# Two transformer blocks on one core: weights with adjacent column blocks, a later way back of the expert pairs, and row parts made without a copy

## The chip, the cores and the metric

The kernel runs on one core of a Trainium2 chip. The metric is the time of one execution in microseconds of device time; the runs shown are three, and their median is used. A core has TensorE (PE, with PEld for its weight loads), VectorE (DVE), ScalarE (ACT), GpSimd (POOL) and SyncE (SP), which here issues nearly all DMA transfers.

## The reference, cut to what matters

A first block (stick-breaking attention and a spatial gating unit, then a mixture of 32 experts) is followed by a second block (differential attention, sparse attention, a cross attention over a memory, and a table of 16384 small experts). There are 256 tokens of width 1024, all in 32-bit floats. What the change touches most is the mixture:

```python
def hierarchical_moe(x, ...):                      # x: 256 rows, normed
    ...                                            # top-1 group of 4, then top-2 of its 8 experts, for each token
    for g in range(N_GROUPS):                      # 4
        h = jax.nn.silu(jnp.einsum('nd,edf->nef', xt, w_gate[g])) * jnp.einsum('nd,edf->nef', xt, w_up[g])
        out = out + jnp.einsum('nef,efd->nd', h * combine[:, g, :, None], w_down[g])
```

An expert has `w_gate` and `w_up` of 1024 x 512 and `w_down` of 512 x 1024, 2 MiB each.

## The kernel before, in words

The program is written in program order against tiles with a fixed number of buffers; a planner orders the instructions of each engine by its own estimates and gives out the buffers, and `after(a, b)` makes it keep `a` behind `b` on an engine.

Weights come by SyncE in tiles of 128 x 2048 floats (1 MiB): `queue` lists them, `fill` (L86) issues a load whenever there is room, `next_w` (L128) takes the next one. In the expert stage 11 such tiles are in rotation (pools of 7, 3 and 1). The first pair has three of its tiles in `act` buffers and two in the `hi` and `lo` buffers besides.

Routing (L521 to L613): the rows `X` are scaled by `rs` into `xs` (ACT, L536), copied to the rounded upper part `xsh` (ACT, L537), and the rest `xsl` is taken by POOL (L538). In `route`, DVE makes the masks, PE counts slots (L585, L586), and `slots` (L615) builds `P`, a 0/1 matrix that says which token sits in which of an expert's 64 places. `slots` builds it in two halves of four experts.

Experts (`moe`, L688): four groups g of eight experts, each as four pairs. For each group `gather` (L706) multiplies `xsh` and `xsl` by `P`, which gives the experts' inputs `xe` transposed, in eight blocks of 128 columns of the model width; `gather(0)` serves the first two pairs and stands ahead of the group, `gather(1)` stands in the second pair. Each pair then has: gate and up, 64 matmuls of 512 columns into the `acc` banks (L757; two experts side by side, 64 columns of the array each); `mo_s` from both (ACT L760, DVE L761); four transposes (L765) and the copy `mo_h` (ACT L767); 32 down matmuls into the `oacc` banks (L779); the parts `yh` (ACT L787) and `yl` (DVE L788); and the way back (L789 to L796), eight matmuls with `PT`, the transposed `P`, and four additions to `X` on DVE. `yh`, `yl`, `P` and the parts of other weights share the `hi` and `lo` buffers, three each. PSUM scratch is `wk`, four banks. `memory` (L801) is worked off in pieces behind the pairs 2 to 6 and brings four weight tiles of its own.

The contraction index is laid out so that partition q holds the rows 8q to 8q+7 of a weight (`_cols`, L1686). So the matching block k of the activations has the columns k, 8+k, 16+k and so on, and is read with a step of 8 elements ("(q k) -> k q"): L206 (`xpair`), L644, L703 and L704 (`vh`, `vl`, the stationary operand of the gather) and L1362 (`peer`). For `w_down`, with four blocks, `sv` (L764) is read with a step of 4. Other weights (`_rows`, L1692) already have adjacent blocks.

Of the kernel before, what the change touches and what calls it, by code (L numbers as in the profile page):

```python
# [17 lines left out]
ALU = mybir.AluOpType  # L18
# [24 lines left out]
class _Kernel:  # L43
# [180 lines left out]
    def norm_rows(self, rows, rs, dst):  # L224
        for j in range(2):
            self.nc.vector.tensor_scalar(dst[:, j, :], rows[:, j, :], rs[:, j:j + 1], None, op0=ALU.mult)
# [89 lines left out]
    def phase_a(self):  # L316
# [231 lines left out]
    def route(self, lg):  # L548
# [39 lines left out]
        self.P = {0: self.slots(0)}  # L588
# [26 lines left out]
    def slots(self, g):  # L615
# [3 lines left out]
        for e in range(0, 8, 4):  # L619
            for j in range(2):  # L620
# [6 lines left out]
    def overflow(self):  # L627
# [9 lines left out]
        with tc.If(n > CAP):  # L637
# [6 lines left out]
            xr = xs.rearrange("p j (q k) -> p j k q", k=8)  # L644
# [5 lines left out]
            with tc.For_i(0, 32, 1) as e:  # L650
# [13 lines left out]
                for j in range(2):  # L664
# [4 lines left out]
                    sv = s.rearrange("p (f k) -> p k f", k=4)  # L669
# [18 lines left out]
    def moe(self):  # L688
# [9 lines left out]

        for g in range(4):
# [3 lines left out]
            vh = self.xsh.rearrange("p j (q k) -> p j k q", k=8)  # L703
            vl = self.xsl.rearrange("p j (q k) -> p j k q", k=8)  # L704
# [40 lines left out]
            for pr in range(4):  # L745
                p = g * 4 + pr
                ps = {}
                for nm in ("w_gate", "w_up"):
                    ps[nm] = self.acc()
                    for kh in range(2):  # L750
# [3 lines left out]
                        for k in range(4):  # L754
                            for e in range(2):
                                s0 = (pr * 2 + e) * CAP
                                nc.tensor.matmul(ps[nm][e * 64:(e + 1) * 64, :], lhsT=xe[kh][:, k, s0:s0 + CAP],  # L757
                                                 rhs=w[e][:, k, :], start=(kh + k == 0), stop=(kh * 4 + k == 7))
# [4 lines left out]
                sv = s.rearrange("p (f k) -> p k f", k=4)  # L763
# [25 lines left out]
                for hf in range(2):  # L789
                    sl = slice(hf * 512, (hf + 1) * 512)  # L790
# [962 lines left out]
```

## Time and profile before

| what | before |
|---|---|
| three runs, us | 1798.29, 1800.45, 1802.6; median 1800.45 |
| the profiled execution, us | 1797.24 |
| its span, us | 1795.5 |
| mean granted TensorE clock | 0.988 |
| PE / DVE / ACT / POOL busy | 96% / 55% / 38% / 17% |
| moved by DMA | 410 MB, mean 228 GB/s |
| expert stage | 141.2 to 674.1 us of the span |

How to read it: times are counted from the span's start. A busy share says how long an engine had at least one instruction under way, not that it ran at its peak; matmuls overlap, so that the distance between two starts tells more than the duration of one. A wait names the instruction that waited and the one that released it; "issue" is time without a wait that the trace shows. PEld loads a stationary operand while PE works on the one before. `out<-in` gives the tiles by the program's names, for a matmul the moving operand first, then the stationary one. In tables by stretch the columns are: the stretch, its length, then busy time with the number of instructions in brackets for PE, PEld, DVE, ACT and POOL, then the granted clock of TensorE as a share of 2.4 GHz, the mean busy share of the 16 DMA engines, and what they moved.

### The profile page before, as it was taken

Reading aid. Unit: us, or ns where it says so; the run is one execution under the profiler, and the core shown is the slowest. Engines: PE = TensorE matmul, PEld = TensorE weight load, DVE = VectorE, ACT = ScalarE, POOL = GpSimd, SP = SyncE. Lnnn points to the kernel's source line nnn. Section 1 sums busy time; section 2 is a strip of 40 time slices with the busy share of each in tenths; the row PEclk is TensorE's granted clock in tenths of the full one; section 3 lists DMA queues with packets and bytes.
Section 4 is the critical chain, followed back from the end, with each engine's and each line's share of the span. In section 5 each row is a group of like instructions: output and inputs, shape, how many; then the busy total and the mean of one; then the engine's idle time right before and its main releaser. Section 6 shows DMA issues by size and latency. Waiting matters only on the chain. (4 is left out here: it accounts for less than half of the span.)

```text
span 1795.5 us, 27447 instructions
## 1 busy us (share of the span) xinstructions
PE 1718.2 (96%) x11096; PEld 1354.5 (75%) x11096; DVE 982.3 (55%) x2008; ACT 683.0 (38%) x1150; POOL 309.9 (17%) x178
## 2 busy tenths in 40 slices
PE   8999999999999998999999889999999999999998
PEld 7984445544434438888989889999999978888886
DVE  5462232212212116667566999999999944444444
ACT  6551121111101115546455444544444444444443
POOL 4321000000000005321537620000000022222221
PEclk9998999999999999999999989999999999999999
DMA  9527898898999978352215444444444455565553
GB/s 371 216 110 287 322 415 338 351 382 359 381 416 382 388 325 328 127 212 91 99 38 176 141 144 156 150 157 147 160 165 146 165 175 200 190 232 200 188 188 117
DMA packets 69250, 410.02 MB, mean 228 GB/s; under 512 B 9216, under 2 KB 9856, under 8 KB 28544
## 3 DMA queue, kind: packets, MB, share of 16 engines
q1 hardware_dynamic: 67840, 406.64, 60.4%
q8 instruction: 88, 1.44, 0.3%
q10 hardware_dynamic: 1280, 1.59, 0.2%
q14 instruction: 42, 0.34, 0.1%
HBM read 406.11 MB, written 2.10 MB: 227 GB/s over the span
## 5 line engine op out<-in xcount | busy, mean ns | idle before, releaser
L145 ACT ACTIVATE hi<-w 128x1024 fp32r<-128x1024 f32 x368 | 388.9, 1060 | 504.5 <-PE oa L155 176.9
L146 DVE TENSOR_TENSOR lo<-w,hi 128x1024 fp32r<-128x1024 f32 x260 | 327.2, 1260 | 222.0 <-ACT hi L145 221.7
L146 POOL TENSOR_TENSOR lo<-w,hi 128x1024 fp32r<-128x1024 f32 x108 | 267.2, 2476 | 1018.4 <-ACT hi L145 928.0
L155 PE MATMUL acc<-act,lo 128*128 128x256 f32 x928 | 267.0, 288 | 5.8 <-DVE lo L146 5.8
L153 PE MATMUL acc<-act,hi 128*128 128x256 f32 x928 | 266.3, 287 | 2.4 <-ACT hi L145 1.3
L154 PE MATMUL acc<-act,hi 128*128 128x256 f32 x928 | 264.0, 285 | 0.0
L757 PE MATMUL acc<-w,act 128*64 128x512 f32 x1016 | 246.6, 597 | 0.0
L154 PE MATMUL acc<-lo,act 128*128 128x256 f32 (+1 forms) x592 | 197.1, 333 | 3.0 <-POOL lo L146 1.6
L155 PE MATMUL acc<-hi,act 128*128 128x256 f32 (+1 forms) x592 | 195.8, 333 | 0.2 <-DVE act L1265 0.2
L155 PEld LDWEIGHTS acc<-act,lo 128*128 128x128 f32 x928 | 178.1, 192 | 9.3 <-DVE lo L146 6.6
L153 PEld LDWEIGHTS acc<-act,hi 128*128 128x128 f32 x928 | 178.3, 192 | 6.3 <-ACT hi L145 2.2
L153 PE MATMUL acc<-hi,act 128*128 128x256 f32 (+1 forms) x592 | 177.7, 335 | 1.8 <-ACT act L1608 1.0
L154 PEld LDWEIGHTS acc<-act,hi 128*128 128x128 f32 x928 | 178.3, 192 | 1.4 <-issue 1.2
L757 PEld LDWEIGHTS acc<-w,act 128*64 128x64 f32 x1016 | 73.3, 137 | 135.2 <-issue 131.3
L153 PE MATMUL oa<-act,hi 128*128 128x256 f32 x528 | 151.8, 288 | 4.0 <-ACT hi L145 3.9
L155 PE MATMUL oa<-act,lo 128*128 128x256 f32 x528 | 152.7, 289 | 0.0
L154 PE MATMUL oa<-act,hi 128*128 128x256 f32 x528 | 150.8, 286 | 0.0
L1498 DVE SCALAR_TENSOR_TENSOR oha<-cols,iT,g 128x384 bf16<-128x384 bf16 x256 | 142.3, 612 | 0.0
L154 PEld LDWEIGHTS acc<-lo,act 128*128 128x128 f32 x592 | 114.1, 193 | 16.5 <-DVE lo L146 3.5
L153 PEld LDWEIGHTS acc<-hi,act 128*128 128x128 f32 x592 | 114.1, 193 | 13.3 <-ACT act L1608 1.2
L155 PEld LDWEIGHTS acc<-hi,act 128*128 128x128 f32 x592 | 113.8, 193 | 10.6 <-DVE act L1265 0.4
L779 PE MATMUL oa<-w,mo_h 128*64 128x512 f32 x480 | 113.1, 599 | 5.0 <-ACT mo_h L767 5.0
(424 smaller groups left out, 2587.6 us busy)
## 6 DMA issues: line engine op xcount, KB each, us to landing
w<-w_gate SPq DMA_DIRECT2D x64, 1024.0 KB, 8.5
w<-peer_u SPq DMA_DIRECT2D x64, 1024.0 KB, 4.9
w<-peer_v SPq DMA_DIRECT2D x64, 1024.0 KB, 4.9
w<-w_up SPq DMA_DIRECT2D x63, 1024.0 KB, 9.5
w<-w_down SPq DMA_DIRECT2D x60, 1024.0 KB, 8.7
w<-w_in SPq DMA_DIRECT2D x28, 1024.0 KB, 9.2
w<-w_out SPq DMA_DIRECT2D x8, 1024.0 KB, 16.1
w<-peer_wq SPq DMA_DIRECT2D x8, 1024.0 KB, 4.8
```

Source lines behind the costliest of these rows:

```text
L145: self.last_hi = nc.scalar.activation(hi, src, AF.Copy)
L146: r = (nc.gpsimd if gp else nc.vector).tensor_tensor(lo, src, _f(hi), op=ALU.subtract)
L153: first = mm(ps, lhsT=a[0], rhs=b[0], start=start, stop=False)
L154: mm(ps, lhsT=a[0], rhs=b[1], start=False, stop=False)
L155: return first, mm(ps, lhsT=a[1], rhs=b[0], start=False, stop=stop)
L757: nc.tensor.matmul(ps[nm][e * 64:(e + 1) * 64, :], lhsT=xe[kh][:, k, s0:s0 + CAP], rhs=w[e][:, k, :], start=(kh + k == 0), stop=(kh * 4 + ...
L779: nc.tensor.matmul(y[hf][e * 64:(e + 1) * 64, :], lhsT=hT[:, kh * 2 + k, e * 64:(e + 1) * 64], rhs=w[e][k][:, hf * 512:(hf + 1) * 512], st ...
L1498: V.scalar_tensor_tensor(ab[:, t], cols[:, None, :].to_broadcast([128, 3, 128]), iT[:, t0 + t:t0 + t + 1], g3[:, :, t0 + t:t0 + t + 1].to_ ...
```

## The change

Three edits. First, the host lays every weight out by `_cols`, now with partition q of block k holding row 128k + q; `_rows` is gone, `w_gate`, `w_up`, `w_down`, `w_gb_2` and `peer_u_2` are permuted to match, and the gains are turned (`turned`; `final_norm_g` has a second copy, `final_norm_gk`). On the chip each "(q k)" becomes "(k q)" and each "(f k)" becomes "(k f)": blocks of 128 adjacent columns. Shapes and numbers of the transfers stay. (`norm_rows` and `softmax_rows` are renamed.) Second, the way back of a pair is kept in `late` and issued in the next pair: its first half (columns 0 to 511) behind the last up matmul and ahead of the transposes of `mo_s`, its second half behind the transposes, both pinned there with `after`; the last pair's stands behind the loop. Third, `xs` is gone: `xsh` is made by one scaled ACT copy of `X`, and `xsl` by DVE from `X`, `rs` and `xsh`, pinned between the two halves of the first `P`.

```diff
@@ xpair; the same edit in overflow, moe (vh, vl) and peer
-        r = rows.rearrange("p j (q k) -> p j k q", k=8)
+        r = rows.rearrange("p j (k q) -> p j k q", k=8)
@@ phase_a
-        xs = self.act().rearrange("p (j d) -> p j d", j=2)
...
         for j in range(2):
-            nc.scalar.activation(xs[:, j], X[:, j], AF.Copy, scale=rs[:, j:j + 1])
-            nc.scalar.activation(self.xsh[:, j], xs[:, j], AF.Copy)
-            nc.gpsimd.tensor_tensor(self.xsl[:, j], xs[:, j], _f(self.xsh[:, j]), op=ALU.subtract)
-        self.route(lg)
+            nc.scalar.activation(self.xsh[:, j], X[:, j], AF.Copy, scale=rs[:, j:j + 1])
+        self.route(lg, rs)
@@ route
-        self.P = {0: self.slots(0)}
+        def low():
+            for j in range(2):
+                z = V.scalar_tensor_tensor(self.xsl[:, j], self.X[:, j], rs[:, j:j + 1], _f(self.xsh[:, j]),
+                                           op0=ALU.mult, op1=ALU.subtract)
+                self.after(z, self.last_P)
+
+        self.P = {0: self.slots(0, low)}
@@ slots
         for e in range(0, 8, 4):
+            if e and between:
+                between()
@@ moe
+        late = []
+
+        def back_to(yh, yl, PT, pr, hf, after=None):
+            sl = slice(hf * 512, (hf + 1) * 512)
+            for j in range(2):
+                bk = self.wk()
+                lt = PT[:, pr, j * 128:(j + 1) * 128]
+                mm = nc.tensor.matmul(bk, lhsT=lt, rhs=yh[:, sl], start=True, stop=False)
+                if after:
+                    self.after(mm, after)
+                after = nc.tensor.matmul(bk, lhsT=lt, rhs=yl[:, sl], start=False, stop=True)
+                nc.vector.tensor_tensor(X[:, j, sl], X[:, j, sl], bk, op=ALU.add)
+            return after
...
+                if late:
+                    mm = back_to(*late, 0, mm)
                 pt = self.wk()
-                sv = s.rearrange("p (f k) -> p k f", k=4)
+                sv = s.rearrange("p (k f) -> p k f", k=4)
                 for k in range(4):
-                    nc.tensor.transpose(pt[:, k * 128:(k + 1) * 128], sv[:, k, :], self.ident)
+                    tr = nc.tensor.transpose(pt[:, k * 128:(k + 1) * 128], sv[:, k, :], self.ident)
+                    if late and not k:
+                        self.after(tr, mm)
                 ht = self.tmp([128, 512], "mo_h")
                 nc.scalar.activation(ht, pt, AF.Copy)
+                if late:
+                    back_to(*late, 1, tr)
...
-                for hf in range(2):
-                    sl = slice(hf * 512, (hf + 1) * 512)
-                    for j in range(2):
-                        bk = self.wk()
-                        lt = PT[:, pr, j * 128:(j + 1) * 128]
-                        nc.tensor.matmul(bk, lhsT=lt, rhs=yh[:, sl], start=True, stop=False)
-                        nc.tensor.matmul(bk, lhsT=lt, rhs=yl[:, sl], start=False, stop=True)
-                        nc.vector.tensor_tensor(X[:, j, sl], X[:, j, sl], bk, op=ALU.add)
+                late = yh, yl, PT, pr
                 if 0 <= p - M0 < 5:
                     next(memory)
+        for hf in range(2):
+            back_to(*late, hf)
@@ _cols (the old body of _rows; _rows goes)
-    return np.ascontiguousarray(w.reshape(128, k // 128, m // n, n).transpose(2, 0, 1, 3)).reshape(m // n, 128, -1)
+    return np.ascontiguousarray(w.reshape(k // 128, 128, m // n, n).transpose(2, 1, 0, 3)).reshape(m // n, 128, -1)
@@ layout
+    turned = lambda g: c(g.reshape(8, 128).T).reshape(-1)
...
-        r[n] = a[n].reshape(32, 128, -1)
+        r[n] = c(a[n].reshape(32, -1, 128, a[n].shape[-1]).transpose(0, 2, 1, 3)).reshape(32, 128, -1)
```

## Rows read from the trace of the kernel before

**Rows 1.** Busy us by group of pairs; last columns granted clock, DMA share, GB/s

```profile
141.20:271.90 130.70, 128.17 (x586) 61.95 (x587) 33.48 (x73) 21.94 (x40) 3.15 (x2) 0.98 0.85 339
271.90:417.30 145.40, 139.78 (x667) 72.08 (x665) 28.26 (x47) 20.59 (x34) 8.17 (x3) 1.00 0.91 362
417.30:545.30 128.00, 122.73 (x520) 55.90 (x520) 25.22 (x45) 13.34 (x24) 0.00 (x0) 0.99 0.94 383
545.30:674.10 128.80, 121.86 (x520) 55.68 (x521) 25.59 (x43) 16.38 (x28) 2.28 (x1) 1.00 0.89 360
```

**Rows 2.** Waits of PE and PEld, 140 to 675 (us in total, times, longest)

```profile
PE wk L765 <- DVE mo_s L761: 12.0, 13, 0.9
PE oa L779 <- ACT mo_h L767: 5.0, 7, 0.7
...
PEld wk L794 <- ACT yh L787: 11.5, 15, 0.8
...
PEld acc L757 <- DMA w<-w_down: 0.8, 3, 0.3
```

**Rows 3.** Timeline of one plain pair (start us, duration us, engine, line)

```profile
492.57 13.95 PE L757 MATMUL acc<-w,act 128*64 128x512 f32 x62
...
506.63 0.75 DVE L761 SCALAR_TENSOR_TENSOR mo_s<-acc,mo_c,mo_s 128x512 f32<-128x512 f32 x1 [12.63 <-PE acc L757]
...
507.43 0.75 PE L765 MATMUL wk<-ident,mo_s 128*128 128x128 f32 x4 [0.92 <-DVE mo_s L761]
...
508.93 7.14 PE L779 MATMUL oa<-w,mo_h 128*64 128x512 f32 x32 [0.75 <-ACT mo_h L767]
...
519.38 13.95 PE L757 MATMUL acc<-w,act 128*64 128x512 f32 x62
```

**Rows 4.** Ten us of that pair, columns as in Rows 1

```profile
510.00:520.00 10.00, 10.00 (x44) 4.05 (x41) 3.32 (x6) 1.19 (x2) 0.00 (x0) 1.00 1.02 424
```

**Rows 5.** Weight loads by shape, 140 to 675 (busy us, mean ns, idle before)

```profile
L713 PEld LDWEIGHTS wk<-P,act 128*128 128x128 f32 x128 | 37.1, 338 | 0.0
...
L795 PEld LDWEIGHTS wk<-yl,mo_PT 128*128 128x128 f32 x64 | 10.6, 188 | 8.9 <-DVE X L796 3.2 <-DVE yl L788 2.7 <-issue 1.6
...
L765 PEld LDWEIGHTS wk<-ident,mo_s 128*128 128x128 f32 x64 | 9.0, 209 | 24.4 <-DVE mo_s L761 23.4 <-issue 0.8
...
L730 PEld LDWEIGHTS wk<-ident,P 128*128 128x128 f32 x32 | 3.7, 143 | 0.0
```

**Rows 6.** Timeline of a gather's loads and of contiguous matmuls

```profile
473.56 0.58 PEld L711 LDWEIGHTS wk<-P,act 128*128 128x128 f32 x2
474.04 0.58 PEld L713 LDWEIGHTS wk<-P,act 128*128 128x128 f32 x2
...
386.04 0.28 PE L154 MATMUL acc<-lo,act 128*128 128x256 f32 x1
386.15 0.28 PE L155 MATMUL acc<-hi,act 128*128 128x256 f32 x1
```

**Rows 7.** A wait of ACT in 240 to 430

```profile
ACT hi L145 <- PE wk L794: 2.1, 1, 2.1
```

**Rows 8.** Timeline of POOL and DVE ahead of the first gather

```profile
136.12 4.65 POOL L538 TENSOR_TENSOR act<-act,act 128x1024 fp32r<-128x1024 f32 x2 [4.59 <-ACT act L537]
...
136.26 2.29 DVE L579 TENSOR_TENSOR msk<-oh,oh 128x64 f32<-128x64 f32 x1
...
139.56 1.82 DVE L621 TENSOR_TENSOR P<-iota,slot 128x256 fp32r<-128x256 f32 x2
...
141.52 0.76 DVE L621 TENSOR_TENSOR P<-iota,slot 128x256 fp32r<-128x256 f32 x2
```

**Rows 9.** Timeline of SyncE's weight loads near the stage's start

```profile
125.84 2.03 SPq L122 DMA_DIRECT2D w<-w_gate  x4
155.55 4.24 SPq L122 DMA_DIRECT2D w<-w_up  x4
```

**Rows 10.** Ten us around that gather, columns as in Rows 1

```profile
470.00:480.00 10.00, 9.09 (x33) 6.38 (x33) 1.72 (x3) 2.01 (x4) 0.00 (x0) 0.83 1.01 422
```

More of the change, by code (lines that the diff above doesn't have):

```diff
@@ L222, in flip, with norm_cols @@
         return r
-    def norm_rows(self, rows, rs, dst):
+    def norm_cols(self, rows, rs, dst):
         for j in range(2):
@@ L546, in queue_pair, with route @@
             self.queue(w[a], pool=at.get(a))
-    def route(self, lg):
+    def route(self, lg, rs):
         nc, V = self.nc, self.nc.vector
@@ L613, in route, with slots @@
         V.tensor_copy(self.most, most[:1])
-    def slots(self, g):
+    def slots(self, g, between=None):
         P = self.hl.tile([128, 1024], F32R, tag="hi", name=self.nm("P"), bufs=self.n_hi)
@@ L643, in overflow @@
             nc.vector.tensor_tensor(xs, _f(self.xsh), _f(self.xsl), op=ALU.add)
-            xr = xs.rearrange("p j (q k) -> p j k q", k=8)
+            xr = xs.rearrange("p j (k q) -> p j k q", k=8)
             for k in range(8):
@@ L702, in moe @@
             xe = [self.act().rearrange("p (k s) -> p k s", k=4) for _ in range(2)]
-            vh = self.xsh.rearrange("p j (q k) -> p j k q", k=8)
-            vl = self.xsl.rearrange("p j (q k) -> p j k q", k=8)
+            vh = self.xsh.rearrange("p j (k q) -> p j k q", k=8)
+            vl = self.xsl.rearrange("p j (k q) -> p j k q", k=8)
             def gather(hf):
@@ L756, in moe @@
                                 s0 = (pr * 2 + e) * CAP
-                                nc.tensor.matmul(ps[nm][e * 64:(e + 1) * 64, :], lhsT=xe[kh][:, k, s0:s0 + CAP],
-                                                 rhs=w[e][:, k, :], start=(kh + k == 0), stop=(kh * 4 + k == 7))
+                                mm = nc.tensor.matmul(ps[nm][e * 64:(e + 1) * 64, :], lhsT=xe[kh][:, k, s0:s0 + CAP],
+                                                      rhs=w[e][:, k, :], start=(kh + k == 0), stop=(kh * 4 + k == 7))
                 s = self.tmp([128, 512], "mo_s")
@@ L838, in gains_c @@
         a, self.g2 = [self.cst.tile([128, 8], F32, tag="g_" + nm, name="g_" + nm) for nm in ("mix", "2")]
-        for g, nm in ((a, "norm_mix_2"), (self.g2, "final_norm_g")):
+        for g, nm in ((a, "norm_mix_2"), (self.g2, "final_norm_gk")):
             self.nc.scalar.dma_start(g, self.I[nm].rearrange("(p k) -> p k", k=8))
@@ L902, in phase_c @@
         rsb2 = rsb[:, None, :].to_broadcast([128, 2, 256])
-        self.norm_rows(xs, r1, X)
+        self.norm_cols(xs, r1, X)
         self.save("X", lambda o: nc.sync.dma_start(o.rearrange("(j p) d -> p j d", p=128), X))
@@ L1688, in _cols @@
     k, m = w.shape
-    return np.ascontiguousarray(w.reshape(128, k // 128, m // n, n).transpose(2, 0, 1, 3)).reshape(m // n, 128, -1)
-def _rows(w, n):
-    k, m = w.shape
     return np.ascontiguousarray(w.reshape(k // 128, 128, m // n, n).transpose(2, 1, 0, 3)).reshape(m // n, 128, -1)
@@ L1704, in layout @@
         r[n] = a[n].reshape(-1)
+    turned = lambda g: c(g.reshape(8, 128).T).reshape(-1)
+    r["final_norm_gk"] = turned(r["final_norm_g"])
+    for n in ("attn_norm_g", "ffn_norm_g", "norm_mix_2", "norm_mem_2", "norm_ffn_2"):
+        r[n] = turned(r[n])
     r["mix_norm_g"] = c(np.concatenate([a["sb_out_norm_g"].reshape(-1), a["sg_out_norm_g"].reshape(-1)])
@@ L1722, in layout @@
     r["w_in_2"] = _cols(np.concatenate([w[:, :o[3]], qb, kv, w[:, o[6]:]], axis=1))
-    r["w_gb_2"] = c(w[:, o[5]:o[6]]).reshape(128, -1)
+    r["w_gb_2"] = _cols(w[:, o[5]:o[6]], 24)[0]
     for n in ("nsa_ck_w1_2", "nsa_cv_w1_2"):
@@ L1729, in layout @@
     for n in ("w_branch_a_2", "w_cross_o_2"):
-        r[n] = _rows(a[n][0], 512)
-    r["w_branch_b_2"] = _rows(a["w_branch_b_2"][0].reshape(2, 4, 64, D).transpose(1, 0, 2, 3).reshape(512, D), 512)
-    r["w_out_2"] = _rows(a["w_out_2"][0], 256)
-    r["w_cross_q_2"] = _rows(a["w_cross_q_2"][0], 256)
+        r[n] = _cols(a[n][0], 512)
+    r["w_branch_b_2"] = _cols(a["w_branch_b_2"][0].reshape(2, 4, 64, D).transpose(1, 0, 2, 3).reshape(512, D), 512)
+    r["w_out_2"] = _cols(a["w_out_2"][0], 256)
+    r["w_cross_q_2"] = _cols(a["w_cross_q_2"][0], 256)
     r["w_cross_kv_2"] = _cols(a["w_cross_kv_2"][0])
```

16 lines of the change are left out of this document (8 added, 8 removed).

## The prediction

> **What bounds the kernel now.** I read the table by stage first [rows 1]. The expert stage (141.2 to 674.1 us: four expert groups of four pairs, 532.9 us) is where two of the three edits lie; the stages before and behind it keep their work. PE is busy over 94% of it, and the DMA engines 85 to 94%: two limits close together, and the forecast turns on both. Which one rules now is in the waits [rows 2]: PE's weight loader waited 0.8 us for weights from memory in all, but the transposes waited 12.0 us for `mo_s`, the down matmuls 5.0 us for `mo_h`, the way back's weight loads 11.5 us for `yh`. So PE sets the pace, and the transfers follow it. Then one plain pair, with neither gather nor memory work in it [rows 3]: 62 gate and up matmuls from 492.57, transposes at 507.43, down at 508.93, the way back behind its end at 516.07, next pair at 519.38. The pair takes 26.81 us; 12 weight tiles of 1 MiB at the full rate (424 GB/s at a share of 1.02, [rows 4]) take 12 x 2.473 = 29.7 us. Plain pairs already outrun the transfers and live on the 11 tiles of buffer; the pairs with gathers and memory work let the transfers catch up.
>
> **Column blocks adjacent.** On the chip this changes no size, no count and no DMA: the host permutes rows of the weights, and blocks that were read with a step of 8 floats (`vh`, `vl`, rows in `xpair`, `peer`) or 4 floats (`sv`) become runs of 128. What gets cheaper is the weight load of TensorE where such a block is stationary. The gather is the large one: 128 + 128 matmuls of 256 columns, with a weight load of 338 ns; the way back's loads, same type and size but contiguous, take 188 ns [rows 5]. In sequence, a gather's loads go in pairs 0.48 us apart (473.56, 474.04), so 0.24 us for one matmul; contiguous matmuls of the same 256 columns start 0.11 to 0.12 us apart (386.04, 386.15) [rows 6]. 256 x (0.24 - 0.115) = 32 us of PE. The eviction (0.47 us for each four matmuls, two engines in turns) doesn't limit: four matmuls will take 0.46. Bounds: 0, if the step is not why the loads are long, to 256 x 0.135 = 35. I take 32, since the type and the tile are equal in both rows and only the step differs. The 64 transposes of `mo_s` have loads of 209 ns against 143 for those of `P` [rows 5]; in sequence 0.14 against about 0.115, so 64 x 0.025 = 1.6 us (0 to 4). The Trainium skill (SBUF — State Buffer, the note on cachelines under Door 1: The DMA port swizzle) says that reads are at full speed while two hits fall on one 16-byte line, so that a step of 4 floats is free and one of 8 is not. For the gather that is what the row shows; for `mo_s` the row (209 against 143) speaks against it, and by the page these 1.6 us would be 0. The other transposes, 16 each in four places outside the stage, lie beside evictions of 0.47 us a block; I count them at nothing, 2 us at most if the evictions weren't there.
>
> **Way back pinned into the next pair.** The same 128 matmuls, 64 adds on DVE and no DMA; they only move, in the queues of PE and DVE alone (SyncE's and POOL's are not passed). Removed: down ends at 516.07, the next pair's long run starts at 519.38, and of that 0.43 is two early gate matmuls. With the block gone, gate matmuls follow down at once (the two `acc` banks were read long before). So 3.1 us less. Put back: four matmuls (about 0.23 each, twice 256 columns) between the last up matmul and the transposes, four behind these. Now the gap from the end of up (492.57 + 13.95 = 506.52) to down (508.93) is 2.41 us, with 0.5 of transposes in it [rows 3]. The first four take 0.92 while DVE makes `mo_s` (it lasts 0.75), the last four 0.92 while ACT copies `mo_h`: 1.84 of work into 1.9 us of waiting. Down starts as before; the pair gains the 3.1. What this needs: the four `wk` banks, of which the fifth user waits for the first add of DVE (0.64 us each); DVE's queue has `mo_s` first, then four adds, and nobody waits for the last ones. Not every pair has the whole gap: in about seven, gathers or the memory's matmuls fill part of it already (13 of 16 transposes waited for `mo_s`, only 7 for `mo_h`, [rows 2]). 9 x 3.1 + 7 x 0.5 = 31, less a price: `yh` and `yl` now hold a slot of three for most of a pair more, and the splits of the memory's weights and the next `P` need the same slots. One split already waited 2.1 us for a way back [rows 7]; four such blocks come, so 1 to 8 us; I take 2 in the sum. Net 29; bounds 16 x 0.5 - 8 = 0 and 50.
>
> **Scaled rows' parts.** Removed: two ACT copies off the chain, and two POOL subtractions of 2.3 us each. While POOL ran them (136.12 to 140.77), DVE's `msk` of 64 columns took 2.29 us and two builds of `P` 1.82 [rows 8]; alone these are 0.2 and 0.76, as the next two builds show. So 3 us come off the way to the first gather. Added: two DVE operations of 1024 columns, about 1.2 us each (as the split's subtraction on DVE in the page's groups), between the halves of `P`; the lower part of the first gather waits for them, the upper doesn't, and behind them queue the second half of `P`, `comb` and half of the gather's evictions. Bounds -1 and +3, I take +1. One `act` tile less changes no load of the first pair that I can see.
>
> **The sum.** PE: 32 + 1.6 + 29 + 1 = 63.6 us; by PE alone the stage ends at 674.1 - 63.6 = 610.5. The transfers: when PE starts on the experts, 16 tiles are there; 180 of the 196 (192 of experts, 4 for the memory) are still to come, 180 x 2.473 = 445 us. The first of these is issued when the first gate tiles are free, now at 155.55 [rows 9], then near 149. With 2.4 us until the first bytes arrive (4.9 from issue to landing of a tile in the page's DMA issues, less 2.47), the last lands no sooner than 597 to 603, and behind it stand 16 down matmuls and the last way back, now 666.6 to 674.1, so 7.5 us: 604 to 611. Both limits fall together, so neither hides behind the other: in plain pairs (23.7 us of PE against 29.7) the buffer drains by 6 us each, and PE will wait for weights, which it didn't before. From a walk through the pairs with 11 tiles I estimate 4 to 10 us for that; I take 6. Gain 58: the stage ends near 616. Profiled execution (1797.24; span 1795.5) to 1739; the median of the runs shown is 3.2 above it, so 1742 on the measure.
>
> **The rivals.** (1) The step isn't what the gather's loads cost: PE gains 31, the transfers hide nothing, 1800 - 31 = 1769. For it: nothing in the rows but that no step of another size stands beside; against it 338 to 188 at equal shape. (2) The transfers rule earlier than worked out: each wait of PE frees tiles late, and the queue has gaps where it now has a share of 0.85 to 0.94. If the stage keeps the mean rate of its best group, 383 GB/s [rows 1], 180 tiles take 493 us and it ends near 652: 1778; halfway, 1760. (3) Waiting for weights lowers PE's clock. From 470 to 480 the mean grant is 0.83 [rows 10], so 3.4 us at 1.2 instead of 2.4 GHz, after PE had waited for `mo_s` and was on a gather. Such an episode costs 1.7 us of PE; one for each pair costs 27: 1769. (4) Slower than before: the same mechanism all through the expert stage. At half the clock the 62 and 32 matmuls of a pair (13.95 + 7.14 us, [rows 3]) take 42 us, more than the 29.7 of transfers, so PE rules again, and 16 pairs cost 16 x 21 = 337 us; it decides from 34 episodes of 1.7 us on, two in each pair, and three give 1742 + 48 x 1.7 = 1824. Against it: in 510 to 520 the transfers are at their limit and the clock is whole [rows 4]. (5) Memory gives no more over a long stretch than it gives now, a mean of 361 GB/s over the four groups [rows 1]: then every us that PE gains is waited for, and the time is 1800. Against it: 383 over the third group and 424 over 10 us. The Trainium skill (DMA: Bandwidth & Descriptors, Specifications) states such a limit, about 358 GB/s of HBM for a core; by that the stage's 205.5 MB would take 574 us, more than the stage has now, so the trace disagrees.
>
> **How the numbers follow.** Forecast 0.72, (1) 0.07, (2) 0.10, (3) 0.06, (4) 0.03, (5) 0.02. The forecast's own range: the way back from half my value up to the point where the transfers' ceiling of 70 us stops any gain, the gather within 3 us, waits for weights of 4 to 10 us: 1729 to 1760. To hold 8 in 10 it takes in (1): 1728 to 1769. Within 0.2% (3.6 us, about what a measurement here can tell from no change) only (5): 0.02; slower (4): 0.03; faster 0.95.
>
> **What would show it.** Gather weight loads near 190 ns and matmuls 0.12 apart: else step one is wrong. Waits of transposes for `mo_s` and of down for `mo_h` near 0, no wait for `yh`, and the next pair's gate right behind down: else the way back is. `msk` at 0.2 us and no POOL work near it: the third. PE waiting for weights by 5 to 10 us and a share of DMA at 0.97 or more over the stage: the meeting of the limits; with no such wait and a later end than 616, PE lost time I have not seen. Wrong would make it above all a planner that, with other estimates, orders the memory's work and the gathers otherwise.

## The result and the profile after

| what | before | after |
|---|---|---|
| median of all executions, us | 1800.1 | 1756.7 |
| lowest and highest, us | 1798.3, 1802.6 | 1754.6, 1758.0 |
| the profiled execution, us (its span) | 1797.24 (1795.5) | 1757.5 (1755.8) |
| expert stage, first gather to the last matmul of the last way back, us | 141.2 to 672.4 | 136.2 to 631.1 |

(The prediction's end of the stage, 674.1, is the first matmul of the stage behind it.)

The ratio is 0.9757 (95% interval 0.9740 to 0.9774), a gain of 43.7 us on 1800. The forecast was 1742, so the direction and the place were right and the gain was 14 us smaller than said. Gains below are ratios times 1800 us, each against executions of the kernel before on the same chip; the bounds of the intervals are given with them. One execution of the run with the memory's pieces from pair 6 took 3354.5 us and counts in no comparison.

First the table by stage of the changed kernel, the four expert groups, columns as in [rows 1]:

```profile
136.20:257.90 121.70, 119.53 (x579) 55.84 (x580) 32.25 (x69) 21.82 (x40) 3.11 (x2) 0.96 0.90 362
257.90:398.20 140.30, 137.00 (x667) 66.25 (x665) 29.01 (x48) 20.01 (x33) 7.26 (x3) 0.99 0.95 377
398.20:510.10 111.90, 111.90 (x523) 50.80 (x521) 25.20 (x45) 13.37 (x24) 0.00 (x0) 1.00 1.01 417
510.10:634.00 123.90, 117.39 (x539) 52.21 (x537) 28.05 (x48) 18.32 (x31) 3.60 (x2) 1.00 0.97 402
```

Against [rows 1] the groups gained 9.0, 5.1, 16.1 and 6.0 us (the last one to the end of the way back). The groups are alike in their work, except that groups 0 and 1 have the memory's pieces besides; so the uneven gains are the thing to explain. Group 2 is what the forecast promised. Group 1 fell short with TensorE at work, group 3 with the transfers at their limit.

Second, the waits of PE and PEld in 134 to 640 (total, times, longest), the counterpart of [rows 2]:

```profile
PEld acc L153 <- ACT hi L145: 6.7, 4, 2.5
PEld acc L777 <- DMA w<-w_up: 6.3, 4, 2.2
...
PE acc L777 <- DMA w<-w_up: 3.5, 3, 1.3
PE acc L153 <- ACT hi L145: 3.2, 3, 1.6
...
PEld wk L787 <- DVE mo_s L781: 2.9, 13, 0.2
...
PEld oa L805 <- ACT mo_h L791: 2.5, 7, 0.4
...
PEld wk L712 <- ACT yh L813: 0.8, 1, 0.8
```

PE's waits for `mo_s` and `mo_h` (12.0 and 5.0 us before) are gone as forecast; what is left of such waits is the loader's 2.9, 2.5 and, for `yh`, 0.8 us (11.5 before). Two others took their place: for weights (forecast), and of the memory's products (L153) for the split of their weights on ACT (L145), which before showed only as a remark on slots.

Third, the weight loads (busy us, mean ns, idle before) that answer to [rows 5]:

```profile
L731 PEld LDWEIGHTS wk<-P,act 128*128 128x128 f32 x128 | 20.8, 200 | 19.0 <-issue 17.0 <-ACT act L738 1.6
L733 PEld LDWEIGHTS wk<-P,act 128*128 128x128 f32 x128 | 20.8, 200 | 0.5 <-DVE act L588 0.5
...
L787 PEld LDWEIGHTS wk<-ident,mo_s 128*128 128x128 f32 x64 | 6.9, 141 | 4.6 <-DVE mo_s L781 2.9 <-issue 0.8 <-DVE X L716 0.8
```

The gather's went from 338 to 200 ns, those of the transposes of `mo_s` from 209 to 141. Last the timeline of PE in a plain pair ([rows 3]) and in the last pair:

```profile
486.64 13.95 PE L777 MATMUL acc<-w,act 128*64 128x512 f32 x64
500.52 0.50 PE L712 MATMUL wk<-yh,mo_PT 128*128 128x512 f32 x1
...
501.56 0.61 PE L787 MATMUL wk<-ident,mo_s 128*128 128x128 f32 x4
...
503.03 7.14 PE L805 MATMUL oa<-w,mo_h 128*64 128x512 f32 x32
...
599.59 4.45 PE L777 MATMUL acc<-w,act 128*64 128x512 f32 x18
605.22 3.65 PE L777 MATMUL acc<-w,act 128*64 128x512 f32 x16 [1.18 <-DMA w<-w_gate]
610.19 3.65 PE L777 MATMUL acc<-w,act 128*64 128x512 f32 x16 [1.31 <-DMA w<-w_up]
615.17 3.65 PE L777 MATMUL acc<-w,act 128*64 128x512 f32 x14 [1.32 <-DMA w<-w_up]
```

The plain pair runs without a gap: gate and up, half of the way back, transposes, the other half, down, 23.4 us where it took 26.81. In the last pair the same 64 gate and up matmuls take 19.2 us instead of 13.9, because each block behind the first waits for its tile.

One number is no effect of the change. The changed kernel's profiled execution reaches the routing's first transposes at 130.21 us, the kernel before at 132.87. In the profiled executions of all kernels below, with either layout, they come at 132.6 to 134.1. The granted clock shows why: every one of these other executions has 3.4 us or more at half the clock between 20 and 130 us (the kernel before a mean of 0.83 from 100 to 120), and the changed kernel's has none there. The number of such stretches differs between executions of one kernel: the mean clock of the changed kernel's four is 0.989, 0.988, 0.989 and 0.987. So these 2.7 us are one execution's luck, and I compare lengths of groups, which do not contain them. A stretch of 3.4 us at half the clock costs 1.7 us, so a difference of that size between two groups can be luck as well.

### The profile page after: what moved, and what is told of

The parts are those of the page before. It is cut to its first block, busy times and chain, and to the rows that moved or that the text cites. A ratio compares the mean times of both kernels' runs of the same rounds, so it can differ in the third digit from the quotient of the medians.

```text
span 1755.8 us, 27472 instructions
## 1 busy us (share of the span) xinstructions
PE 1687.8 (96%) x11096; PEld 1330.7 (76%) x11096; DVE 981.4 (56%) x2010; ACT 680.9 (39%) x1148; POOL 304.9 (17%) x176
## 5 line engine op out<-in xcount | busy, mean ns | idle before, releaser
L145 ACT ACTIVATE hi<-w 128x1024 fp32r<-128x1024 f32 x368 | 388.9, 1059 | 506.3 <-PE oa L155 180.6
L153 PE MATMUL acc<-act,hi 128*128 128x256 f32 x928 | 267.7, 289 | 4.0 <-ACT hi L145 2.8
L153 PEld LDWEIGHTS acc<-act,hi 128*128 128x128 f32 x928 | 179.6, 194 | 9.4 <-ACT hi L145 5.5
L777 PEld LDWEIGHTS acc<-w,act 128*64 128x64 f32 x1016 | 80.4, 137 | 139.3 <-issue 126.4
L153 PE MATMUL acc<-hi,act 128*128 128x256 f32 (+1 forms) x592 | 177.3, 334 | 3.6 <-ACT hi L145 1.6
L153 PE MATMUL oa<-act,hi 128*128 128x256 f32 x528 | 151.7, 287 | 4.0 <-ACT hi L145 3.9
L153 PEld LDWEIGHTS acc<-hi,act 128*128 128x128 f32 x592 | 113.4, 192 | 16.7 <-ACT hi L145 3.6
L154 PEld LDWEIGHTS acc<-lo,act 128*128 128x128 f32 x592 | 113.4, 192 | 16.3 <-DVE lo L146 3.3
L805 PE MATMUL oa<-w,mo_h 128*64 128x512 f32 x480 | 125.0, 599 | 0.0
```

The source lines that it names most:

```text
L145: self.last_hi = nc.scalar.activation(hi, src, AF.Copy)
L153: first = mm(ps, lhsT=a[0], rhs=b[0], start=start, stop=False)
L154: mm(ps, lhsT=a[0], rhs=b[1], start=False, stop=False)
L777: mm = nc.tensor.matmul(ps[nm][e * 64:(e + 1) * 64, :], lhsT=xe[kh][:, k, s0:s0 + CAP], rhs=w[e][:, k, :], start=(kh + k == 0), stop=(kh * ...
L805: nc.tensor.matmul(y[hf][e * 64:(e + 1) * 64, :], lhsT=hT[:, kh * 2 + k, e * 64:(e + 1) * 64], rhs=w[e][k][:, hf * 512:(hf + 1) * 512], st ...
```

## The experiments

Two theories stood at first. Theory A: the forecast sized the edits rightly on TensorE, and the missing 14 us went where the transfers become the limit. Theory B: the edits themselves are worth less.

### One edit at a time

The kernel before with the first edit alone:

```diff
-            vh = self.xsh.rearrange("p j (q k) -> p j k q", k=8)
+            vh = self.xsh.rearrange("p j (k q) -> p j k q", k=8)
... (all of the layout; way back and route as before)
```

> The kernel before with the first edit alone (column blocks adjacent). Theory A (the gains of the edits on TensorE are as large as worked out, and what is missing in sum is lost where the transfers become the limit): this edit alone still leaves TensorE as the bound, so it gives its whole 33.6 us: 1766.5 us, or 2 to 3 us less if the 2.65 us by which the changed kernel is ahead of before at the routing come from this edit too. Theory B (the steps were mis-sized on TensorE itself): 20 to 28 us, so 1772 to 1780.

Measured: ratio 0.9814 (0.9795 to 0.9833), 33.5 us less (30.1 to 36.9); median 1765.7. The groups of this kernel:

```profile
140.91:265.26 124.35, 121.60 (x587) 54.52 (x587) 33.38 (x73) 21.71 (x40) 3.17 (x2) 0.99 0.90 361
265.26:402.42 137.16, 131.56 (x666) 63.74 (x664) 28.22 (x47) 20.50 (x34) 8.16 (x3) 1.00 0.95 384
402.42:521.81 119.39, 114.11 (x521) 47.48 (x521) 25.19 (x45) 13.26 (x24) 0.00 (x0) 1.00 1.00 411
521.81:640.83 119.02, 113.85 (x520) 47.40 (x520) 23.91 (x41) 14.79 (x26) 0.51 (x1) 1.00 0.94 391
```

This is theory A. The groups gain 6.3, 8.2, 8.7 and 8.0 us: each about its 64 gather matmuls times 0.125, group 0 less. Their sum is 31.2, and the gather's 256 matmuls alone, summed from each start to the next, take 37.9 us instead of 67.1. So the forecast's step holds to 2 or 3 us; that the times agree to 0.1 us is chance.

The kernel before with the second edit alone:

```diff
-                for hf in range(2): ... (way back behind yl)
+                if late: mm = back_to(*late, 0, mm)      # behind up
+                if late: back_to(*late, 1, tr)           # behind the transposes
+                late = yh, yl, PT, pr
```

> The kernel before with the second edit alone (way back of a pair in the next pair), the blocks read with a step of 8 and 4 as before. Theory A: 29 us alone, 1771; with the first edit alone that is a sum of over 60, and the two together fall short of it. Theory B (the way back gains less, since the memory's products now wait for their splits and each switch between kinds of matmul costs time that was counted at nothing): 10 to 18 us, 1782 to 1790, and the single gains add up to about the 43 us of the three together.

Measured: ratio 0.9884 (0.9859 to 0.9909), 20.9 us less (16.4 to 25.4); median 1777.6. Between the theories, nearer to B. Its groups:

```profile
142.18:269.23 127.05, 125.50 (x579) 62.03 (x579) 30.91 (x69) 21.91 (x40) 3.16 (x2) 0.97 0.86 345
269.23:411.55 142.32, 138.21 (x666) 71.97 (x665) 28.92 (x48) 20.09 (x33) 7.18 (x3) 1.00 0.92 367
411.55:531.51 119.96, 119.96 (x523) 58.96 (x521) 25.22 (x45) 13.37 (x24) 0.00 (x0) 1.00 0.96 392
531.51:652.28 120.77, 120.68 (x530) 60.56 (x528) 26.25 (x44) 15.74 (x27) 0.74 (x1) 1.00 0.99 408
```

Groups 2 and 3 gain 8.1 and 6.2, together 14.3; the forecast's count for them (four plain pairs at 3.1, four with gathers at 0.5) is 14.4. Groups 0 and 1 gain 3.6 and 3.1, where the count gave 14.6 after its price of 2. So about 8 us are missing, all in the two groups that have the memory's work. PE waits there 3.2 us for the upper parts of the splits and 2.5 for the lower ones, and from 260 to 270 us, behind the first of these waits, the mean clock is 0.83, so 3.4 us at half, which cost 1.7. So of the 10 us that the price comes to with the 2 in the count, 7.4 stand in the rows.

The kernel before with the third edit alone:

```diff
-            nc.scalar.activation(xs[:, j], X[:, j], AF.Copy, scale=rs[:, j:j + 1])
-            nc.scalar.activation(self.xsh[:, j], xs[:, j], AF.Copy)
-            nc.gpsimd.tensor_tensor(self.xsl[:, j], xs[:, j], _f(self.xsh[:, j]), op=ALU.subtract)
+            nc.scalar.activation(self.xsh[:, j], X[:, j], AF.Copy, scale=rs[:, j:j + 1])
... (low() between the halves of the first P)
```

> The kernel before with the third edit alone (upper and lower parts of the scaled rows straight from X, no work for POOL). Forecast: the first gather starts 2 to 4 us earlier (msk at 0.2 us instead of 2.29, two builds of P at 0.76 instead of 1.82), the lower parts cost up to 3 of it, so 0 to 3 us less in all: 1797 to 1800. Rival: POOL was not what held msk and P, and their durations stay at 2.29 and 1.82 us.

Measured: ratio 1.0013 (1.0003 to 1.0023), 2.3 us slower (0.5 to 4.1). What it should do it does. From its timeline of DVE, which answers to [rows 8]:

```profile
136.37 0.22 DVE L576 TENSOR_TENSOR msk<-oh,oh 128x64 f32<-128x64 f32 x1
...
137.61 0.76 DVE L627 TENSOR_TENSOR P<-iota,slot 128x256 fp32r<-128x256 f32 x2
...
138.85 2.47 DVE L588 SCALAR_TENSOR_TENSOR act<-X,rs,act 128x1024 fp32r<-128x1024 f32 x2
```

From the routing's transposes to the first gather it takes 5.99 us instead of 8.33. That is lost again later: group 1 lasts 152.3 us instead of 145.4, with a wait of 2.8 us for a split on DVE and a stretch of half clock behind it at 410.7, neither of which the kernel before has there.

### All but one edit

The changed kernel with the third edit undone:

```diff
-            nc.scalar.activation(self.xsh[:, j], X[:, j], AF.Copy, scale=rs[:, j:j + 1])
+            nc.scalar.activation(xs[:, j], X[:, j], AF.Copy, scale=rs[:, j:j + 1])
... (and the rest of the lines just shown, back as before; low() goes)
```

> The changed kernel with the third edit undone (first and second edits alone). Theory A, from the run of the third edit alone (2.3 us slower than before): also in the sum this edit gives nothing, and without it the time is 1753 to 1757. Rival: its earlier first gather (138.9 against 141.2 us) pays, once the waits behind it go another way: without it 1758 to 1761.

Measured: ratio 0.9745 (0.9727 to 0.9763), median 1753.6 (1752.4 to 1755.2) against the changed kernel's 1756.7 (1754.6 to 1758.0). So the third edit gives nothing in the sum either and most likely costs 2 to 3 us, though the two intervals of the ratio overlap. Its groups:

```profile
141.51:260.64 119.13, 117.39 (x578) 53.40 (x579) 30.82 (x69) 21.81 (x40) 3.16 (x2) 0.99 0.89 362
260.64:394.92 134.28, 130.16 (x667) 63.83 (x665) 28.84 (x48) 19.90 (x33) 7.17 (x3) 1.00 0.98 395
394.92:506.82 111.90, 111.90 (x523) 50.81 (x521) 25.22 (x45) 13.38 (x24) 0.00 (x0) 1.00 1.01 416
506.82:628.08 121.26, 115.67 (x530) 51.26 (x528) 26.23 (x44) 15.71 (x27) 0.72 (x1) 1.00 0.98 407
```

This is the run that tells where gains add up. Gains by group against before:

| | group 0 | group 1 | group 2 | group 3 |
|---|---|---|---|---|
| first edit alone | 6.3 | 8.2 | 8.7 | 8.0 |
| second edit alone | 3.6 | 3.1 | 8.1 | 6.2 |
| their sum | 9.9 | 11.3 | 16.8 | 14.2 |
| both together | 11.6 | 11.1 | 16.2 | 5.7 |

In three groups the edits add up to within 1.7 us. The whole loss of their meeting, 8.5 us, lies in group 3, where PE waits 5.5 us for weights and the transfers move 407 GB/s. By times it is the same, 33.5 + 20.9 - 45.9 = 8.5, though the bounds of the three ratios together leave some 6 us either way.

What the third edit costs in this pair of kernels is seen in group 1 (140.3 with it, 134.3 without). The larger part is the planner's order of the second gather among the down matmuls. The changed kernel, down matmuls alone (gather matmuls stand between the rows):

```profile
318.00 1.93 PE L805 MATMUL oa<-w,mo_h 128*64 128x512 f32 x4
...
320.53 3.65 PE L805 MATMUL oa<-w,mo_h 128*64 128x512 f32 x12
...
325.72 1.07 PE L805 MATMUL oa<-w,mo_h 128*64 128x512 f32 x2
...
327.40 1.07 PE L805 MATMUL oa<-w,mo_h 128*64 128x512 f32 x2
...
329.07 3.65 PE L805 MATMUL oa<-w,mo_h 128*64 128x512 f32 x12
...
332.70 0.39 PE L153 MATMUL acc<-hi,act 128*128 128x256 f32 x1
```

Without the third edit:

```profile
320.26 3.65 PE L799 MATMUL oa<-w,mo_h 128*64 128x512 f32 x16
...
325.94 3.71 PE L799 MATMUL oa<-w,mo_h 128*64 128x512 f32 x16
...
330.63 0.28 PE L153 MATMUL acc<-hi,act 128*128 128x256 f32 x1
```

The same 32 down and 32 gather matmuls take 15.7 us (316.95 to 332.70) in five blocks and 11.4 us (319.21 to 330.63) in two; PE waits for nothing in either. What differs is how the down matmuls start. Without the third edit all 32 start in twos, 0.01 to 0.06 us apart (two experts lie side by side in the array), one such two every 0.43 us. In the changed kernel 16 of the 32 start alone, 0.43 us behind the last, as the two of the block at 325.72 do, which take as long as four would. That is 24 steps instead of 16, 8 x 0.43 = 3.4 of the 4.3 us; the other 0.9 falls on six more changes between gather and down. Most of what is left of the 6 us is clock: from 360 to 370 the grant was 0.86 with the edit and 1.00 without, which can be luck. The third edit touches neither place. That the planner orders them otherwise is seen; why its estimates tip is not settled.

### The load by the step of its block

```diff
-            vh = self.xsh.rearrange("p j (k q) -> p j k q", k=8)
-            vl = self.xsl.rearrange("p j (k q) -> p j k q", k=8)
+            vh = self.xsh.rearrange("p j (h q k) -> p j h k q", h=2, k=4)
+            vl = self.xsl.rearrange("p j (h q k) -> p j h k q", h=4, k=2)
```

> The changed kernel, but in the gather the blocks of the upper part are read with a step of 4 floats and those of the lower part with a step of 2, so that the experts get other columns and the values are other ones. It tells what the weight load of a block costs by its step: 8 in the kernel before (338 ns), 1 in the changed kernel. Theory A, the load takes longer with every doubling of the step: about 290 ns at 4 and 240 at 2. Rival, by the rule of the Trainium skill (SBUF — State Buffer, cachelines) that two hits on one 16-byte line are at full speed: 4 and 2 both as at step 1, near 190 ns, and the whole as the changed kernel.

Measured, 1765.1 us in one execution and these loads (upper part L731 with step 4, lower part L733 with step 2):

```profile
L731 PEld LDWEIGHTS wk<-P,act 128*128 128x128 f32 x128 | 34.8, 321 | 18.8 <-issue 17.0 <-ACT act L738 1.6
...
L733 PEld LDWEIGHTS wk<-P,act 128*128 128x128 f32 x128 | 22.0, 213 | 0.4 <-DVE act L588 0.4
```

So 200 ns at step 1, 213 at 2, 321 at 4, 338 at 8: neither a growth with every doubling nor a free step of 4. What costs lies between 2 and 4. The Trainium skill (SBUF — State Buffer, the note on cachelines under Door 1: The DMA port swizzle) calls a step of 4 floats free; for TensorE's weight load this run contradicts it. The same note's other words, that a line of 16 bytes needs two hits, fit the run: at a step of 2 floats two reads fall on a line, at 4 only one. The step is thereby shown to be the gather's cost: the gather's 256 matmuls, summed from each start to the next, take 13.2 us more than in the changed kernel (51.3 against 38.1), with half of the loads at 321 ns.

### The transfers out of the way

Both kernels without the loads of `w_up`:

```diff
-        for nm in ("w_gate", "w_up", "w_down") ...   for a in range(12)
+        for nm in ("w_gate", "w_down") ...           for a in range(8)
-                        w = [... for z in self.next_w(2)]
+                        if nm == "w_gate": wg[kh] = self.next_w(2)
+                        w = [... for z in wg[kh]]
```

> The kernel before without the loads of w_up: the up matmuls multiply the pair's w_gate tiles instead, so their values are other ones; all instructions on the engines stay, and a pair moves 8 tiles (19.8 us at the full rate) instead of 12. This takes the transfers off as a limit. Both theories: the expert stage lasts as before, 525 to 533 us, since TensorE waited for weights by less than 2 us.

> The changed kernel without the loads of w_up, in the same way (the up matmuls multiply the pair's w_gate tiles, other values). Against the same reduction of the kernel before it shows what the edits save on TensorE with the transfers out of the way. Theory A: the expert stage is 60 to 65 us shorter than in that kernel. Theory B: 42 to 50 us shorter, about as in the whole kernels.

Measured: the stage takes 515.0 us in the kernel before so reduced, 16 less than whole, a miss of both theories; and 470.1 in the changed one, 44.9 less, which is theory B's range. The first number says that this pair does not compare like orders: with fewer loads the planner puts gate matmuls of the next pair into the waits for `mo_s` (3.7 us of them are left instead of 12.0), so a part of the second edit's gain is taken beforehand. What the second does show is groups 2 and 3 of the changed kernel without a shortage of weights:

```profile
386.99:495.93 108.94, 108.94 (x523) 45.12 (x521) 25.18 (x44) 13.36 (x24) 0.00 (x0) 1.00 0.74 295
495.93:609.37 113.44, 111.39 (x530) 46.51 (x528) 26.15 (x44) 15.84 (x27) 4.74 (x2) 1.00 0.67 265
```

Group 3 takes 113.4 us instead of 121.0. But group 2, in which the changed kernel waits for no weights, is 3.0 us shorter too (108.9 for 111.9): in both groups the order is another here, with no down matmul that starts alone (in the changed kernel 16 and 18 do). So some 4.6 of the 7.6 us of group 3 are left to the transfers, as much as the 4.7 us of its waits for weights.

### The memory's products

In the changed kernel the memory's product stands right behind down, and its split comes too late. From the timeline behind pair 3:

```profile
247.97 0.60 ACT L813 ACTIVATE yh<-oa 128x512 fp32r<-128x512 f32 x1 [6.57 <-PE oa L805]
248.46 1.99 ACT L145 ACTIVATE hi<-w 128x1024 fp32r<-128x1024 f32 x2
...
249.56 0.39 PE L153 MATMUL acc<-act,hi 128*128 128x256 f32 x1 [0.79 <-ACT hi L145]
...
250.82 0.39 PE L155 MATMUL acc<-act,lo 128*128 128x256 f32 x1 [0.76 <-DVE lo L146]
```

and the ten us behind it, columns as in [rows 1]:

```profile
250.00:260.00 10.00, 9.24 (x65) 9.18 (x65) 4.07 (x8) 1.84 (x4) 2.41 (x1) 0.83 1.01 418
```

PE waits twice and then gets half the clock (1.2 GHz) for 3.4 us: matmuls 0.21 apart instead of 0.12. The half clock doesn't follow such waits every time: in the changed kernel without the third edit PE waits at the same product 0.79 and 0.76 us, and the clock stays whole. Before, the way back stood between down and the product, and the split was made meanwhile. Four runs on that. The pieces behind later pairs:

```diff
-M0 = 2
+M0 = 6
```

> The changed kernel with the memory's five pieces behind the pairs 6 to 10 instead of 2 to 6 (one number changed, M0). Theory A: in the changed kernel TensorE is behind in groups 0 and 1, where the memory's work stands, so that the transfers pause there (24 us worth between 150 and 390), and in groups 2 and 3 the transfers are at their limit and cannot make it up. Then pieces that stand later let the transfers run through, and the stage ends 6 to 15 us earlier: 1742 to 1751. Rival: the pause comes from the buffers and gathers of every group, or the stage is bound by the sum of the transfers in any order; then within 3 us of the changed kernel, 1754 to 1760.

Measured: ratio 0.9751 (0.9731 to 0.9770), so 1755 of 1800, and a median of 1753.6 for the three executions that count: at the lower edge of the rival's range, and above theory A's. Theory A as put there fell. Group 1 now runs at 421 GB/s and group 3 gets 6.6 us shorter, but group 2, which has the products now, takes 140.3 us. So the pause of the transfers in groups 0 and 1 most likely followed TensorE's own work, and moving that work does not shorten it.

Each piece ahead of its pair's down matmuls, with its weight tile ahead of the down tiles:

```diff
+                if 0 <= p - M0 < 5:
+                    next(memory)
                 yh = self.hl.tile(...)
...
                 late = yh, yl, PT, pr
-                if 0 <= p - M0 < 5:
-                    next(memory)
```

> The changed kernel with each piece of the memory's work ahead of its pair's down matmuls instead of behind them (its weight tile comes ahead of the down tiles in the order of loads), so that ACT can split the weights before the copies yh and while TensorE still has other work. Theory A: in the changed kernel TensorE waits at each of these products for the split, which the way back used to cover, and the half clock follows; that costs about 8 us, and without it the time is 1746 to 1752. Rival: those waits only take the place of waits for the transfers; then within 3 us of the changed kernel, 1754 to 1760.

Measured: ratio 0.9720 (0.9705 to 0.9735), median 1750.0, 6.7 us faster than the changed kernel. PE's waits for the products' upper parts in 140 to 655 us of this kernel:

```profile
PE acc L153 <- ACT hi L145: 0.5, 1, 0.5
```

This one stands behind the stage, which ends at 624.6; in the stage there is none. No stretch of half clock is left between 145 us and the end of the stage. Groups 0 and 1 gain 2.7 and 9.4 us (121.7 to 119.0, 140.3 to 130.9); group 3 gives 2.4 back to waits for weights. Of the 9.4, 4.3 lie in pair 5, from its transposes to the next pair's (39.2 to 34.9): there the planner now puts the gather beside the memory's product, and the five blocks of down told above are gone. So the splits are worth some 8 us in the two groups here, two stretches of half clock among them, and the order 4. Against the run without the third edit, which has the same waits without the five blocks and without half clock behind them, groups 0 and 1 are only 3.6 us shorter (119.1 and 134.3 there).

Both together:

```diff
-M0 = 2
+M0 = 6
... (and next(memory) moved ahead of yh, as above)
```

> The run with the memory's splits ahead of down, with its pieces in the pairs 6 to 10 besides. Theory A: with the waits for splits gone from these products, what is left is that TensorE is behind in the first half and the transfers pause there; then the later place now helps, which it didn't with the waits: 1741 to 1746. Rival: the order doesn't matter, the transfers lose as much in group 2 as they win in groups 0 and 1: 1748 to 1752, as with the pieces in pairs 2 to 6.

Measured: ratio 0.9708 (0.9685 to 0.9730), median 1746.5, 0.5 above theory A's range and below the rival's; the interval overlaps that of the run with the pieces in pairs 2 to 6, so it doesn't decide between the two. Group 2 of the run with pieces from pair 6, and group 2 of this one:

```profile
375.14:515.41 140.27, 136.97 (x666) 66.27 (x665) 29.02 (x48) 19.99 (x33) 7.35 (x3) 0.99 0.96 393
```

```profile
373.53:505.88 132.35, 132.35 (x666) 67.75 (x665) 28.39 (x48) 20.84 (x34) 7.07 (x3) 0.99 0.99 408
```

The same work, PE waits for no weights in either, and each has one stretch of half clock. Of the 7.9 us, 3.3 are waits for splits (140.27 less 136.97; in the other run PE waits for nothing). 4.3 us lie in pair 9, from its transposes to the next pair's (39.2 and 34.9), where PE waits for no split in either run: there the run with the splits behind down has the five blocks of down matmuls again. So it is chance that this difference is as large as the 8 us that the second edit alone lacked.

The other way to the same question, the way back of pairs 2 to 6 issued at once again:

```diff
                 if 0 <= p - M0 < 5:
+                    for hf in range(2):
+                        back_to(*late, hf)
+                    late = []
                     next(memory)
```

> The changed kernel with the way back of the five pairs ahead of a piece of the memory's work (pairs 2 to 6) issued at once behind down, as before, and the other eleven late. Theory A: in these five pairs the late way back gains nothing, since what it frees is a wait for the split of the memory's weights that it used to cover: within 3 us of the changed kernel, 1754 to 1760. Rival, the prediction's count (most of these pairs gain 3.1 us from the late way back): 1762 to 1772.

Measured: ratio 0.9803 (0.9781 to 0.9824), median 1764.5, which is the rival's range. By groups it is not so clear: 124.0, 141.1, 111.9, 120.8, so 2.3 us more in group 0 and 0.8 in group 1, which have one and three of the four products. The rest of the 8 us lies outside of these pairs: 3.9 us later at the first gather, most of it the luck told above, and 1.9 behind the stage, with two more stretches of half clock. Nor do the groups compare like orders: the changed kernel's group 1 has the five blocks of down (4.3 us), and in this run PE waits 2.6 us for the lower part of pair 6's split. Whether the late way back gains anything at the memory's pairs stays open.

Last, this kernel with the third edit undone:

```diff
-            nc.scalar.activation(self.xsh[:, j], X[:, j], AF.Copy, scale=rs[:, j:j + 1])
+            nc.scalar.activation(xs[:, j], X[:, j], AF.Copy, scale=rs[:, j:j + 1])
... (xsh and xsl from xs, as before)
```

> The run with the memory's splits ahead of down and its pieces in the pairs 6 to 10, with the third edit undone besides. Theory A: the third edit costs through the order that the planner makes of the gathers and products behind it, in whatever version: 3 us less than with it, 1742 to 1744.5. Rival: that cost lies in the waits for splits and the order of the one pair in which the changed kernel has them; with the splits ahead the edit's earlier first gather (2.3 us) is left, and without it the time is 1747 to 1750.

Measured: ratio 0.9701 (0.9685 to 0.9717), median 1746.3, as with the edit. Between the two expectations: with the splits ahead of down the third edit costs or gains nothing that these intervals show. So its cost in the changed kernel is most likely no property of the edit but of the order that comes with it. By their ratios this run and the one with the splits ahead and the pieces from pair 6 are 10 and 9 us faster than the changed kernel.

## Why the prediction was right and where it was wrong

| term of the sum | forecast, us | measured, us |
|---|---|---|
| column blocks adjacent | 33.6 | 33.5 |
| way back, net | 29 | 20.9 |
| scaled rows | 1 | -2.2 |
| meeting of the limits | -6 | -8.5 |
| gain | 58 | 43.7 |

The measured terms come from ratios that are each sure to 3 to 5 us, and the last two are differences of such ratios (the meeting from the run without the third edit). The first term was right within that, and its ground as well: type and tile alike in both rows, only the step differs. In rows it is a little less than said: the gather gave 29.2 us where 32 were counted, since 0.24 and 0.115 are the distances in sequence and some matmuls stand farther apart. The step-size run closes rival (1). The 1.6 us for the transposes of `mo_s` were in the right place, too (209 to 141 ns), against the Trainium skill (SBUF — State Buffer, the note on cachelines under Door 1: The DMA port swizzle), which calls their step free.

The way back: the mechanism was right in each of its steps. A plain pair gained 3.4 us (3.1 said), PE's waits for `mo_s` and `mo_h` and nearly all for `yh` are gone, and with the second edit alone the groups without memory work gained 14.3 (14.4 said). What failed is the size of one term, the price at the splits: 1 to 8 us, 2 taken, about 10 measured with the second edit alone (31 counted without a price, 20.9 gained), of which 7.4 are seen in rows as waits and half clock. I had the cause as slots held longer. One split did wait for a slot (3.8 us, until 296.25 in the changed kernel), but PE had gate and up matmuls meanwhile (296.26 to 299.91). The runs show another cause: at the four pairs with a product the way back was the cover under which ACT and DVE split the memory's weights; with the splits moved ahead of down the waits are gone. The step "9 x 3.1" counted pairs by who waits in them and did not ask what was done while PE waited. In the trace before it could have been read: behind pair 3 ACT's split stands at 263.05, the way back's first half on PE from 263.29 to 264.50, the product's first matmul at 264.50, with a wait of 0.5 us in all.

The scaled rows: each line of the forecast came (`msk` 0.22, `P` 0.76, 2.3 us to the first gather), and the sum was still wrong in sign (-2.2, bound -1), in the changed kernel because behind it the planner made another order, in which 16 down matmuls start alone, and perhaps by luck with the clock; with another order (splits ahead of down) no cost is seen. The prediction named such a planner as what would make it wrong above all; it gave it no term.

The meeting of the limits: 4 to 10 said, 8.5 measured, and in the form said: PE waits for tiles (4.7 us in rows, 5.3 in the last pair alone if its length is compared), share of DMA 1.01 in group 2 and 0.97 in group 3. So 5 to 6 of the 8.5 us are seen as waits; the rest is not told apart from order. Rival (2) holds as far as groups 0 and 1 go: with gaps in the queue the whole stage moved 390 GB/s on the mean, near its 383, and its halfway value, 1760, came nearer to the result than the forecast's 1742. As a ceiling it is out: from 390 to 620 the changed kernel moved 419 GB/s on the mean of 230 us:

```profile
390.00:620.00 230.00, 225.33 (x1041) 100.52 (x1040) 50.39 (x89) 26.74 (x48) 0.00 (x0) 1.00 1.01 419
```

With it rival (5) is out. The limit of about 358 GB/s in the Trainium skill (DMA: Bandwidth & Descriptors, Specifications), a core's half of what two share, does not bind this kernel, which runs on one core, in this stretch. Rivals (3) and (4) claimed half clock behind waits for weights; in group 3 of the changed kernel, where PE waits for weights, the grant is 1.00. Half clock came, but behind the waits for splits (two stretches of 3.4 us in groups 0 and 1 behind the first gather, 0.83 and 0.86 in their ten us), and with the same waits it stayed away in the run without the third edit.

The parts failed by 8, 3 and 2.5 us in the same direction, and that is the whole 14 us. The forecast's own range, 1729 to 1760, took the result in by its lower bound for the way back, half of the value. That the cause of the price was another than the one named makes this partly luck. So theory A is right for the first edit and for the meeting of the limits, and theory B for the second edit.

## What to carry to other kernels

Before work is taken out of a wait, list what other engines finish during that wait: the next instruction may be covered by it. Gains of several edits should be added up group by group, for they add where one engine rules and vanish where another limit takes over; a run with one edit at a time shows both at once. An edit whose own lines all come out as planned can still lose time where a planner re-orders work that it does not touch, so compare the order, too, and whether matmuls that ran side by side still do.

## What the runs showed of the hardware

TensorE's load of a 128 x 128 block of floats takes 200 ns in the gather at step 1, 213 at step 2, 321 at step 4 and 338 at step 8; the jump between 2 and 4 was not expected. And two matmuls of 64 columns of the array start together only where the order leaves them side by side: the same 32 down matmuls keep PE busy for 7.36 us where all start in twos, and for 11.35 us where 16 start alone. A change between gather (128 columns) and down (64) costs little beside that, some 0.15 us: six more changes in the longer order, and 0.9 us left for them.
